# Wide products in the first half of the u stage, with the selection cut into half-microsecond steps and finished gates applied first

## The chip, the cores and the metric

The kernel runs as one program on one core of a Trainium2 chip. The metric is device time in microseconds (us) for one execution of the whole program. A core has five engines with instruction queues of their own: PE (TensorE: matrix products; its weight loads are listed as PEld), DVE (VectorE), ACT (ScalarE), POOL (GpSimd) and SP (SyncE, which issues the DMAs here). Each queue is worked off in order, and the queues wait for one another through semaphores.

## The reference, cut to what matters

Two layers run one after the other on 256 tokens of width 1024: a mixer (an SSD mixer, then a retention mixer), an expert FFN, and a gated per-layer input. The change touches the FFN alone, which is the same in both layers:

```python
def peer_ffn(h, w_q, sub_keys, u, v):
    q = (xt @ w_q).reshape(T, PEER_HEADS, 2, PEER_HALF)
    sc = jnp.einsum('thcd,hckd->thck', q, sub_keys)
    s1, i1 = lax.top_k(sc[:, :, 0], K)
    s2, i2 = lax.top_k(sc[:, :, 1], K)
    cand = (s1[..., :, None] + s2[..., None, :]).reshape(T, PEER_HEADS, K * K)
    cand_idx = (i1[..., :, None] * NK + i2[..., None, :]).reshape(T, PEER_HEADS, K * K)
    top_s, top_pos = lax.top_k(cand, K)
    idx = jnp.take_along_axis(cand_idx, top_pos, axis=-1)
    gate = jax.nn.softmax(top_s, axis=-1)
    ...
        hid = jax.nn.gelu(jnp.einsum('tkd,td->tk', u[ib], xb), approximate=False)
        return jnp.einsum('tk,tkd->td', (gb * hid).astype(xb.dtype), v[ib])
```

K is 16, NK is 128 and there are 8 heads: each token chooses 128 of 16384 experts.

## The kernel before, in words

The FFN isn't gathered. The kernel computes all 16384 products of u with every token (the u stage), multiplies them by a gate that is zero for the experts a token did not choose, and multiplies by all of v (the v stage). Float32 accuracy comes from splitting: an operand becomes a high part and a low part of a faster type, and three products are added (high x high, high x low, low x high). ACT writes the high part of a weight block (`wh`), and POOL or DVE subtracts it from the raw block to get the low part (`wl`).

`peer` holds the FFN. The **u stage** is the loop `for i in range(P)`: 128 blocks of 128 experts. A block of u comes in by four DMAs (L513), is transposed by DVE (L516, 128x1024), cast by ACT to `wh` (L521) and subtracted by POOL to `wl` (L524). PE then does 24 products of 256 columns into one PSUM tile `m`: for each of 8 chunks of the width, `wh` with `xh` (L1243) and `wh` with `xl` (L1244), then `wl` with `xh` eight times (L1247). ACT applies the Gelu in the next round (L1207) and so frees the tile; there are two `m` tiles. `get()` hands over the split block of this round and, in the same call, issues the cast and the subtraction for the next block and the load and transpose for the one after it. `wh` and `wl` have two buffers each. The transposed blocks share four raw buffers; from block 56 on (`UEND`) the DMA's target is taken from those four as well.

The first 61 blocks of a layer run beside the **selection**: DVE's top-16 search over the scores, the sums of candidates, the positions, the softmax (an Exp on ACT, L1086) and the experts' numbers. It is a list `bg` of steps with a cost in ns each; `pump(PUMP)` adds 1700 ns of credit per block and pops steps until the credit is used up. Four of the sixteen score pieces are made in rounds 0 and 1 (`score`, L1001 on PE, L1003 on ACT). When `bg` is empty, `sel_tr` turns the results over, and the second half of the u stage begins: for every four tokens `g_hot` makes one-hot tables on DVE (L1172, L1175), `g_lo` scales them on ACT (L1181), `g_mm` multiplies them on PE (L1187) into one of two `g` tiles, and `g_apply` multiplies the gates into H (L1197 on ACT, L1201 on DVE). `g_slot` moves this along by a stage per round. Where gates were there before the hidden value, `times` (L1211) multiplies them in.

The order on each engine is the order in which the Python code calls it; nothing is rearranged afterwards. So within a round before, ACT's order was: cast for the next block, then Gelu of the last block, then `g_apply`'s part, then `g_lo`.

Of the kernel before, what the change touches and what calls it, by code (L numbers as in the profile page):

```python
# [18 lines left out]
P = 128  # L19
# [5 lines left out]
GS = 4096.0  # L25
PUMP = 1700
UEND = 56
# [61 lines left out]
def trunk(ctx: ExitStack, tc: tile.TileContext, a, out, dbg=None, stop=None):  # L89
# [864 lines left out]
    def peer(l, st):  # L954
# [13 lines left out]
        tq = view(S0 + 9344, 256)  # L968
        e1 = A[:, S0 + 9856:S0 + 10368].bitcast(F16).rearrange("p (a b c) -> p a b c", a=4, b=16)
        sel = view(S0 + 10880, 4, 256)  # L970
# [34 lines left out]

        def top(src, scr, ov, oi):

            for r in range(2):
                o8 = slice(8 * r, 8 * r + 8)
                for i in range(2):  # L1010
                    dve.max(ov[i][:, o8], (src, scr)[r][i])
                for i in range(2):
                    dve.max_index(oi[i][:, o8], ov[i][:, o8], (src, scr)[r][i])
                if r == 0:
                    for i in range(2):
                        dve.match_replace(scr[i], ov[i][:, o8], src[i], NEG)

        def sel_codes(tb, c):
            u = 256 * tb + 16 * c
            top([sc[:, tb, c + i] for i in range(2)], sc2, [sv[:, tb, c + i] for i in range(2)],  # L1020
                [iu[:, u + 16 * i:u + 16 * i + 16] for i in range(2)])

        def sel_sums(tb):


            if tb == 0:
                dve.tensor_copy(io16, iota16[:, :16])
# [12 lines left out]

        def sel_cand(tb, h):
            u = 128 * tb + 16 * h
            top([cand[:, tb, h + i] for i in range(2)], cand2, [ts_[:, tb, h + i] for i in range(2)],
                [pu[:, u + 16 * i:u + 16 * i + 16] for i in range(2)])

        def sel_pos(part):

            i, j = pa[:, 0], pa[:, 1]
            if part == 0:
                dve.tensor_copy(si, iu)  # L1050
                dve.tensor_copy(B0, pu)
                dve.tensor_scalar(A2[:, 0].bitcast(U32), pu, 2, None, op0=OP.logical_shift_right)
                dve.tensor_scalar(A2[:, 1].bitcast(U32), pu, 3, None, op0=OP.logical_shift_right)
                dve.tensor_copy(pf, A2.bitcast(U32))
            if part == 1:
                dve.tensor_scalar(A2[:, 0], pf[:, 0], -6.0, 0.0, op0=OP.add, op1=OP.max)
                dve.scalar_tensor_tensor(tq, pf[:, 1], -1.0, A2[:, 0], op0=OP.add, op1=OP.max)
                dve.scalar_tensor_tensor(i, B0, -48.0, tq, op0=OP.add, op1=OP.max)
            if part == 2:
                dve.tensor_scalar(A2[:, 0], i, 8.0, 8.0, op0=OP.mult, op1=OP.add)  # L1060
                dve.tensor_scalar(A2[:, 1], i, 4.0, 24.0, op0=OP.mult, op1=OP.add)
                dve.scalar_tensor_tensor(A2[:, 0], i, 16.0, A2[:, 0], op0=OP.mult, op1=OP.min)
                dve.scalar_tensor_tensor(tq, i, 48.0, A2[:, 1], op0=OP.add, op1=OP.min)
            if part == 3:
                dve.tensor_tensor(tq, tq, A2[:, 0], op=OP.min)
                dve.tensor_sub(j, B0, tq)

        def sel_idx(tb, h, c, part):
            u = slice(128 * tb + 16 * h, 128 * tb + 16 * h + 64)
            if part == 0:  # L1070
                dve.tensor_tensor(e1, io16.unsqueeze(1).unsqueeze(1).to_broadcast([P, 4, 16, 16]),
                                  pa[:, c, u].rearrange("p (a b) -> p a b", a=4).unsqueeze(3).to_broadcast(
                                      [P, 4, 16, 16]), op=OP.is_equal)
            if part == 1:
                s4 = si.rearrange("p (t h c k) -> p t h c k", t=2, h=8, c=2)[:, tb, h:h + 4, c]
                dve.tensor_mul(e1, e1, s4.unsqueeze(2).to_broadcast([P, 4, 16, 16]))
            if part == 2:
                dve.tensor_reduce(sel[:, c, u].rearrange("p (a b) -> p a b", a=4), e1, axis=AX.X, op=OP.add)
# [42 lines left out]
        bg += [(1900, sel_pos, 0), (700, sel_gate), (1100, sel_pos, 1), (1500, sel_pos, 2), (800, sel_pos, 3)]  # L1121
        idx = [(1200, sel_idx, tb, h, c, k) for tb in range(2) for h in (0, 4) for c in range(2) for k in range(3)]
        bg += idx[:3] + [(1400, sel_sum)] + idx[3:6] + [(1000, sel_split)] + idx[6:8]
        for i in range(4):
            bg += [(600, sel_ratio, i), idx[8 + i]]
        bg += idx[12:]
        bg += [(2000, wait), (50, sel_tr, 0), (50, sel_tr, 1)]
        credit = [0.0]
# [8 lines left out]
        def q_fill(k):  # L1137
            if k < 4:
                score(k // 2, k % 2)
            if bg[0][3] < 8:  # L1140
                pump(1550)
            if k < 2:
                q_move(2 * k)
                q_move(2 * k + 1)
            if k in (4, 6):
                xh, xl = split_x(xm[:, 2 * k - 8:2 * k - 4])
                xp.extend((xh[:, i], xl[:, i]) for i in range(4))
            return 0
# [6 lines left out]
        i4 = bank[0][:, :256].bitcast(F16).rearrange("p (a b) -> p a b", b=4)  # L1155
        io16, sm = bank[0][:, 256:272], bank[0][:, 272:288]
        sv2 = bank[0][:, 384:512].rearrange("p (a b) -> p a b", a=8)
# [33 lines left out]
        def g_apply(b, ps, i):  # L1191
# [6 lines left out]
            if i:  # L1198

                for r in ((slice(0, 4), slice(4, P)) if 4 * b + 4 == T else (slice(0, i),)):  # L1200
                    dve.scalar_tensor_tensor(hv[:, r], pv[:, r], 1.0 / GS, hv[:, r], op0=OP.mult, op1=OP.mult)  # L1201
            stored[0] = 4 * b + 4

        def gelu(i, ps):
            st = stored[0]
            if st < T:
# [5 lines left out]

        def g_slot(i, times=lambda: None):

            ap, mm, lo, b = gst["ap"], gst["mm"], gst["lo"], gst["next"]
            gst.update(ap=None, mm=lo, lo=None)
# [5 lines left out]
            if ap:  # L1222
                g_apply(*ap, i)
            if lo:
                g_lo(lo[0], *lo[1])
            times()
            return ap or mm or lo

        last, since = None, 0
        for i in range(P):  # L1230
            wh, wl = get()
            if last is not None:
                g_slot(i, gelu(i - 1, last))
                if bg:
                    pump(PUMP)
                else:
                    since += 1
                    if since % 8 == 0 and T // 4 - gst["next"] > P - 1 - i:
                        g_slot(i)
# [24 lines left out]

        cur = None if open_() else wsplit(0)
        g_slot(P, gelu(P - 1, last))
        while open_():
            g_slot(P)

# [200 lines left out]
```

## Time and profile before

| what | us |
|---|---|
| runs before: median (lowest to highest of 3) | 2180.57 (2179.05 to 2184.51) |
| the profiled execution: its own time | 2179.29 |
| span of the profile | 2177.5 |
| PE busy in the span | 2124.8 |
| u stage, layer 0: first and last start of L1243 | 313.1 to 721.6 |
| v stage, layer 0: first and last start of L1281 | 723.9 to 1072.4 |

The second layer repeats the pattern from about 1371 us on. A line of the timeline gives the start, the duration, the engine, the source line, the operation, the tiles written and read, the shape and how many were merged; in brackets stands how long the engine was idle just before and what ended that. Durations contain an engine's pipeline, so the next instruction often starts before the last one ends; what an engine can do per us is read from the distance of starts.

### The profile page before, as it was taken

To read this page: it belongs to the slowest core of one execution; us is meant where nothing else is said; L and a number is where in the kernel's file an instruction comes from. 1 tells how busy PE (TensorE), PEld (TensorE's weight loads), DVE (VectorE), ACT (ScalarE), POOL (GpSimd) and SP (SyncE) were. 2 spreads that over 40 slices of the span, in tenths; PEclk is the share of its full clock that TensorE was granted. 3 is DMA by queue.
4 is the path that set the end of the run, shared out by engine and by line. 5 is a ranking of instruction groups with operands and counts; after the bars stand their busy time and mean duration, and the time that the engine had idled before them with its cause. 6 is when DMAs were issued, how large, how long until landed. Compare 5 with 4: busy or idle time off the path is not lost. (4 is left out here: it accounts for less than half of the span.)

```text
span 2177.5 us, 39792 instructions
## 1 busy us (share of the span) xinstructions
PE 2124.8 (98%) x15013; PEld 1967.9 (90%) x15013; DVE 1578.6 (72%) x2641; ACT 1207.3 (55%) x2077; POOL 833.5 (38%) x384
## 2 busy tenths in 40 slices
PE   8989999999999999999999999999999999999997
PEld 8978899999999888888898999999999998888887
DVE  7787578888999655555587366989699985555556
ACT  5654444547888544444554444445588874444445
POOL 3242258877777100000033223888777740000001
PEclk9999999999999999999999999999999999999999
DMA  5423577756555655655656456865555556655653
GB/s 185 137 78 98 166 195 194 184 135 167 155 156 154 185 194 194 194 194 193 200 176 186 130 168 184 198 184 151 157 156 156 155 169 193 194 193 194 193 190 121
DMA packets 219577, 370.27 MB, mean 170 GB/s; under 512 B 24240, under 2 KB 163192, under 8 KB 219384
## 3 DMA queue, kind: packets, MB, share of 16 engines
q1 hardware_dynamic: 219064, 367.19, 56.6%
q8 instruction: 118, 1.93, 0.4%
q14 instruction: 75, 0.61, 0.1%
q10 hardware_dynamic: 320, 0.53, 0.1%
HBM read 364.48 MB, written 1.05 MB: 168 GB/s over the span
## 5 line engine op out<-in xcount | busy, mean ns | idle before, releaser
L139 DVE TENSOR_TENSOR wl<-raw,wh 128x1024 fp32r<-128x1024 f32 x379 | 473.5, 1251 | 399.0 <-ACT wh L136 398.7
L136 ACT CAST wh<-raw 128x1024 fp32r<-128x1024 f32 x429 | 450.3, 1052 | 484.3 <-PE ps L1281 359.0
L524 POOL TENSOR_TENSOR wl<-raw,wh 128x1024 fp32r<-128x1024 f32 x256 | 618.3, 2416 | 198.6 <-ACT wh L521 191.1
L1243 PE MATMUL m<-X,wh 128*128 128x256 f32 x2048 | 513.2, 288 | 0.5 <-ACT arena L1207 0.4
L1281 PE MATMUL ps<-wh,X 128*128 128x512 f32 x2048 | 507.3, 389 | 1.9 <-ACT X L1258 1.9
L1244 PE MATMUL m<-X,wh 128*128 128x256 f32 x2048 | 502.0, 283 | 0.0
L1281 PEld LDWEIGHTS ps<-wh,X 128*128 128x128 f32 x2048 | 384.1, 188 | 82.0 <-ACT X L1258 2.3
L521 ACT CAST wh<-raw 128x1024 fp32r<-128x1024 f32 x256 | 269.1, 1051 | 263.2 <-issue 150.1
L1243 PEld LDWEIGHTS m<-X,wh 128*128 128x128 f32 x2048 | 392.2, 192 | 1.0 <-ACT arena L1207 0.9
L1244 PEld LDWEIGHTS m<-X,wh 128*128 128x128 f32 x2048 | 393.0, 192 | 0.0
L199 PE MATMUL ps<-X,wh 128*128 128x256 f32 x2368 | 331.2, 290 | 9.5 <-ACT wh L136 7.9
L341 POOL TENSOR_TENSOR arena<-arena 128x512 f32<-128x512 f32 x15 | 24.1, 1606 | 815.6 <-ACT arena L339 806.5
L199 PEld LDWEIGHTS ps<-X,wh 128*128 128x128 f32 x2368 | 303.8, 195 | 15.5 <-ACT wh L136 9.9
L1247 PE MATMUL m<-X,wl 128*128 128x256 f32 x2048 | 287.4, 283 | 0.1
L1281 PE MATMUL ps<-wl,X 128*128 128x512 f32 x1024 | 274.7, 389 | 0.0
L1247 PEld LDWEIGHTS m<-X,wl 128*128 128x128 f32 x2048 | 264.1, 192 | 0.8 <-POOL wl L524 0.7
L1281 PEld LDWEIGHTS ps<-wl,X 128*128 128x128 f32 x1024 | 192.2, 188 | 39.8
L516 DVE STREAM_TRANSPOSE raw<-raw 128x1024 f32<-128x1024 f32 x144 | 179.0, 1243 | 39.1 <-DMA raw<-in_peer_u 32.7
L139 POOL TENSOR_TENSOR wl<-raw,wh 128x1024 fp32r<-128x1024 f32 x50 | 125.2, 2510 | 182.4 <-ACT wh L136 149.9
L199 PE MATMUL ps<-X,wl 128*128 128x256 f32 x1184 | 178.9, 289 | 7.0 <-POOL wl L139 3.8
L199 PEld LDWEIGHTS ps<-X,wl 128*128 128x128 f32 x1184 | 159.6, 196 | 9.3 <-POOL wl L139 5.0
L1181 ACT ACTIVATE ol<-ol,G 128x128 f16<-128x128 f16 x512 | 162.8, 398 | 0.1
(263 smaller groups left out, 2019.3 us busy)
## 6 DMA issues: line engine op xcount, KB each, us to landing
raw<-in_peer_v SPq DMA_DIRECT2D x256, 512.0 KB, 4.3
raw<-in_peer_u SPq DMA_DIRECT2D x576, 128.0 KB, 3.0
arena<-in_peer_u SPq DMA_DIRECT2D x448, 128.0 KB, 3.3
raw<-in_ret_w_in SPq DMA_DIRECT2D x48, 512.0 KB, 4.0
raw<-in_ssd_w_in SPq DMA_DIRECT2D x41, 512.0 KB, 3.8
raw<-in_peer_w_q SPq DMA_DIRECT2D x32, 512.0 KB, 4.4
raw<-in_ssd_w_out SPq DMA_DIRECT2D x16, 512.0 KB, 3.8
raw<-in_ple_gate SPq DMA_DIRECT2D x16, 512.0 KB, 4.7
```

The lines of the kernel that those rows point to most:

```text
L136: act.copy(wh[:, :n], r[:, :n])
L139: (eng or dve).tensor_sub(wl[:, :n], r[:, :n], wh[:, :n].bitcast(F32))
L199: pe.matmul(self.t[n // 2][:, n % 2], w[:, n * P:(n + 1) * P], x, start=st, stop=sp_, skip_group_check=True)
L341: pool.tensor_add(self.sq[:, 0], self.sq[:, 0], self.sq[:, b])
L516: dve.transpose(t.rearrange("p (k b i) -> p b k i", k=8, b=4), r.rearrange("p (b k i) -> p b k i", k=8, b=4))
L521: act.copy(wh, t)
L524: pool.tensor_sub(wl, t, wh.bitcast(F32))
L1181: act.activation(hl[:, 1, j], hl[:, 0, j], AF.Copy, scale=G1[:, t:t + 1])
L1243: pe.matmul(last, wh[:, s], xh, start=k == 0, stop=False)
L1244: pe.matmul(last, wh[:, s], xl, start=False, stop=False)
L1247: pe.matmul(last, wl[:, s], xh, start=False, stop=k == KD - 1)
L1281: pe.matmul(sums[b], h[:, tb * P:(tb + 1) * P], w[:, n * 512:(n + 1) * 512], start=i == 0 and p == 0, stop=i == P - 1 and p == 2)
```

## The change

In the first half of the u stage (`wide`, while `bg` holds steps) the 16 products of `wh` become 8 of 512 columns, against `xh` and `xl` side by side; the eight of `wl` stay. The two halves of the PSUM tile must then be added: ACT copies the right half to H (L1249 of the changed file), DVE adds the left half (L1250), and the Gelu runs one round later on H in place (L1252). These three, and in the second half the Gelu and `g_apply` and `times` (`g_done`), now stand ahead of `get()`. The selection's steps are cut into pieces, `PUMP` goes from 1700 to 1180, and the experts' numbers come from 32 fused operations and 12 sums of 512 elements in the place of 24 operations on 1024. `warm` loads the Exp table ahead of the Exp.

```diff
-PUMP = 1700
+PUMP = 1180
...
-        def sel_idx(tb, h, c, part):
-            u = slice(128 * tb + 16 * h, 128 * tb + 16 * h + 64)
-            if part == 0:
-                dve.tensor_tensor(e1, io16.unsqueeze(1).unsqueeze(1).to_broadcast([P, 4, 16, 16]),
...
+        def sel_idx(c, r0):
+
+
+            v = pa[:, c].rearrange("p (h k) -> p h k", k=16)
+            for r in (r0, r0 + 1):
+                k = slice(r if c else r // 8 * 8, 16)
+                n = 16 - k.start
+                s1 = si.rearrange("p (h c k) -> p h c k", c=2, k=16)[:, :, c, r:r + 1]
+                dve.scalar_tensor_tensor(e1[:, r, :, k], v[:, :, k], float(r), s1.to_broadcast([P, 16, n]),
+                                         op0=OP.is_equal, op1=OP.mult)
+
+        def sel_add(c, i, h):
+
+            h = slice(h, h + (8, 4)[i])
+            dve.tensor_reduce(sel[:, c].rearrange("p (h k) -> p h k", k=16)[:, h, 8 * i:8 * i + 8],
+                              e1[:, :8 * i + 8, h, 8 * i:8 * i + 8].rearrange("p r h k -> p h k r"), axis=AX.X, op=OP.add)
...
+            act.activation(warm, ident[:, :1], AF.Exp)
...
-        bg = [(3100, sel_codes, tb, c0 + c) for c0 in (0, 8) for tb in range(2) for c in range(0, 8, 2)]
+        bg = [(n, sel_codes, tb, c0 + c, i) for c0 in (0, 8) for tb in range(2) for c in range(0, 8, 2)
+              for i, n in enumerate((400, 520, 520, 400, 520))]
         for tb in range(2):
-            bg += [(1800, sel_sums, tb)]
-            bg += [(2500, sel_cand, tb, h) for h in range(0, 8, 2)]
...
+            bg += [(1300, sel_sums, tb)]
+            bg += [(n, sel_cand, tb, h, i) for h in range(0, 8, 2) for i, n in enumerate((270, 330, 330, 270, 330))]
...
-        last, since = None, 0
+        last, since, wide, late = None, 0, False, None
         for i in range(P):
+            if wide:
+                act.copy(H[:, i - 1], last[:, T:])
+                dve.tensor_add(H[:, i - 1], last[:, :T], H[:, i - 1])
+            if late is not None:
+                act.activation(H[:, late], H[:, late], AF.Gelu)
+            late = i - 1 if wide else None
+            if last is not None:
+                times = gelu(i - 1, last) if not wide else lambda: None
+                g_done(i)
+                times()
             wh, wl = get()
             if last is not None:
-                g_slot(i, gelu(i - 1, last))
+                g_slot()
                 if bg:
                     pump(PUMP)
...
-            last = mis.tile([P, 512], F32, name="m")[:, :T]
-            for k, (xh, xl) in enumerate(xp):
+            last = mis.tile([P, 512], F32, name="m")
+
+            wide = bool(bg)
+            for k, (xh, xl, xx) in enumerate(xp):
                 s = slice(k * P, (k + 1) * P)
-                pe.matmul(last, wh[:, s], xh, start=k == 0, stop=False)
-                pe.matmul(last, wh[:, s], xl, start=False, stop=False)
-            for k, (xh, xl) in enumerate(xp):
+                if wide:
+                    pe.matmul(last, wh[:, s], xx, start=k == 0, stop=k == KD - 1, skip_group_check=True)
+                else:
+                    pe.matmul(last[:, :T], wh[:, s], xh, start=k == 0, stop=False)
+                    pe.matmul(last[:, :T], wh[:, s], xl, start=False, stop=False)
+            for k, (xh, xl, xx) in enumerate(xp):
                 s = slice(k * P, (k + 1) * P)
-                pe.matmul(last, wl[:, s], xh, start=False, stop=k == KD - 1)
+                pe.matmul(last[:, :T], wl[:, s], xh, start=False, stop=k == KD - 1, skip_group_check=wide)
```

How it moves the instructions is seen at three places. First, ACT at the Exp of the selection in layer 0. Before:

```order
L521 CAST wh<-raw 128x1024
L1207 ACTIVATE arena<-m 128x256
L1086 ACT_TABLE_LOAD
L1086 ACTIVATE arena<-arena 128x256
L521 CAST wh<-raw 128x1024
L1207 ACT_TABLE_LOAD
L1207 ACTIVATE arena<-m 128x256
L521 CAST wh<-raw 128x1024
```

And now, at the same place (L1249 is the copy of the right half, L1252 the late Gelu):

```order
L521 CAST wh<-raw 128x1024
L1091 ACT_TABLE_LOAD
L1091 ACTIVATE warm<-ident 128x1
L1094 ACTIVATE arena<-arena 128x256
L1249 COPY arena<-m 128x256
L1252 ACT_TABLE_LOAD
L1252 ACTIVATE arena<-arena 128x256
L521 CAST wh<-raw 128x1024
L1249 COPY arena<-m 128x256
L1252 ACTIVATE arena<-arena 128x256
L521 CAST wh<-raw 128x1024
```

The cast stood between Exp and the Gelu's table load; now the copy, the table load and the Gelu stand ahead of it, as in every round the copy and the Gelu do.

Second, ACT at the first rounds of the u stage as it now is:

```order
L521 CAST wh<-raw 128x1024
L1003 COPY arena<-g 128x512 x2
L1249 COPY arena<-m 128x256
L1252 ACT_TABLE_LOAD
L1252 ACTIVATE arena<-arena 128x256
L521 CAST wh<-raw 128x1024
L1249 COPY arena<-m 128x256
```

Here too the load of the Gelu's table, which stood behind a cast, is ahead of one.

Third, DVE in the second half. Before, a round was transpose, one-hot tables, then the gates:

```order
L516 STREAM_TRANSPOSE raw<-raw 128x4x8x32
L1172 TENSOR_TENSOR oh<-ps,G_98 128x1024
L1175 TENSOR_TENSOR ol<-oh,ps 128x512
L1201 SCALAR_TENSOR_TENSOR arena<-g,arena 128x83x4
L1211 TENSOR_TENSOR arena<-arena,m 128x72
```

The instructions are the same now, but a round begins with the gates:

```order
L1215 SCALAR_TENSOR_TENSOR arena<-g,arena 128x83x4
L1225 TENSOR_TENSOR arena<-arena,m 128x72
L516 STREAM_TRANSPOSE raw<-raw 128x4x8x32
L1186 TENSOR_TENSOR oh<-ps,G_98 128x1024
L1189 TENSOR_TENSOR ol<-oh,ps 128x512
```

On PE nothing changes place: both programs turn the selection over (`sel_tr`) after 61 blocks of a layer, and both multiply the first gates ahead of block 64.

## Rows read from the trace of the kernel before

**Rows 1.** The page, part 1: busy us, share of the span, instructions.

```profile
PE 2124.8 (98%) x15013; PEld 1967.9 (90%) x15013; DVE 1578.6 (72%) x2641; ACT 1207.3 (55%) x2077; POOL 833.5 (38%) x384
```

**Rows 2.** Windows, layer 0's first half: us; PE, PEld, DVE, ACT, POOL busy; clock; DMA.

```profile
313.10:487.80 174.70, 174.70 (x1460) 174.70 (x1459) 152.42 (x458) 84.84 (x125) 142.83 (x60) 1.00 0.66 171
```

**Rows 3.** Timeline of PE: narrow products, first half of the u stage.

```profile
480.01 1.12 PE L1247 MATMUL m<-X,wl 128*128 128x256 f32 x8
...
488.65 1.12 PE L1247 MATMUL m<-X,wl 128*128 128x256 f32 x8
```

**Rows 4.** Timeline of PE: the v stage's last twelve products of 512 columns.

```profile
1069.95 0.62 PE L1281 MATMUL ps<-wh,X 128*128 128x512 f32 x2
...
1072.67 0.64 PE L1319 MATMUL g<-X,wh 128*128 128x256 f32 x4
```

**Rows 5.** Waits, 485 to 540 us, and 1545 to 1600 alike: total, times, longest.

```profile
PE g L1187 <- DVE arena L1201: 1.6, 1, 1.6
```

**Rows 6.** Timeline, first half: ACT's cast, then POOL's subtraction.

```profile
370.81 1.05 ACT L521 CAST wh<-raw 128x1024 fp32r<-128x1024 f32 x1 [1.55 <-issue]
...
371.94 2.41 POOL L524 TENSOR_TENSOR wl<-raw,wh 128x1024 fp32r<-128x1024 f32 x1 [0.47 <-ACT wh L521]
```

**Rows 7.** Timeline at the u stage's end: ACT waits for PE.

```profile
721.80 1.12 PE L1247 MATMUL m<-X,wl 128*128 128x256 f32 x8
722.96 0.17 ACT L1207 ACTIVATE arena<-m 128x4 f32<-128x4 f32 x1 [2.72 <-PE m L1247]
```

**Rows 8.** Timeline: PE's weight load waits for POOL.

```profile
489.90 2.39 POOL L524 TENSOR_TENSOR wl<-raw,wh 128x1024 fp32r<-128x1024 f32 x1 [1.92 <-ACT wh L521]
...
492.35 1.02 PEld L1247 LDWEIGHTS m<-X,wl 128*128 128x128 f32 x8 [0.22 <-POOL wl L524]
```

**Rows 9.** Timeline of ACT: two reads of PSUM, one behind the other.

```profile
508.25 0.37 ACT L1207 ACTIVATE arena<-m 128x256 f32<-128x256 f32 x1
508.52 0.37 ACT L1197 ACTIVATE arena<-g 128x252 f32<-128x252 f32 x1
```

**Rows 10.** Timeline of ACT at the selection's Exp.

```profile
425.30 0.42 ACT L1086 ACTIVATE arena<-arena 128x256 f32<-128x256 f32 x1
425.62 1.03 ACT L521 CAST wh<-raw 128x1024 fp32r<-128x1024 f32 x1
426.67 1.28 ACT L1207 ACT_TABLE_LOAD   x1
427.96 0.38 ACT L1207 ACTIVATE arena<-m 128x256 f32<-128x256 f32 x1
```

**Rows 11.** Timeline, round 2: last score copy; low products of block 2.

```profile
322.77 0.59 ACT L1003 COPY arena<-g 128x512 f32<-128x512 f32 x1 [0.31 <-PE g L1001]
...
324.49 1.12 PE L1247 MATMUL m<-X,wl 128*128 128x256 f32 x8
```

**Rows 12.** Timeline of DVE: sums, transpose, a candidates' step (378.93 to 380.67).

```profile
376.32 0.29 DVE L1029 COPY ps<-arena 128x128 f32<-128x128 f32 x1
...
377.77 1.23 DVE L516 STREAM_TRANSPOSE raw<-arena 128x1024 f32<-128x1024 f32 x1
378.93 0.31 DVE L1011 MAX8 arena<-arena 128x8 f32<-128x64 f32 x2
...
380.67 1.23 DVE L516 STREAM_TRANSPOSE raw<-arena 128x1024 f32<-128x1024 f32 x1
```

**Rows 13.** Timeline of DVE: 256 columns out of PSUM, then a transpose.

```profile
434.80 0.43 DVE L1093 TENSOR_TENSOR ps<-arena,ps 128x256 f32<-128x256 f32 x1
435.14 1.24 DVE L516 STREAM_TRANSPOSE raw<-arena 128x1024 f32<-128x1024 f32 x1
```

**Rows 14.** Lines of DVE, 300 to 510 us: one of the three selections' operations.

```profile
L1078 DVE TENSOR_REDUCE arena<-arena 128x64 f32<-128x1024 f16 x8 | 9.5, 1191 | 0.0
```

**Rows 15.** Timeline of DVE past block 56: transposes that wait for their DMA.

```profile
487.45 1.25 DVE L516 STREAM_TRANSPOSE raw<-raw 128x1024 f32<-128x1024 f32 x1 [0.72 <-DMA raw<-in_peer_u]
...
493.31 1.25 DVE L516 STREAM_TRANSPOSE raw<-raw 128x1024 f32<-128x1024 f32 x1 [0.59 <-DMA raw<-in_peer_u]
```

More of the change, by code (lines that the diff above doesn't have):

```diff
@@ L1003, in score, with top, sel_codes @@
             act.copy(sc[:, tb, 4 * c4:4 * c4 + 4], ps.rearrange("p (a b) -> p a b", a=4))
[L1006 to L1010, printed above, removed]
+        def top(src, scr, ov, oi, part):
+            r = part // 3
+            o8 = slice(8 * r, 8 * r + 8)
+            for i in range(2):
+                if part % 3 == 0:
                     dve.max(ov[i][:, o8], (src, scr)[r][i])
-                for i in range(2):
+                elif part % 3 == 1:
                     dve.max_index(oi[i][:, o8], ov[i][:, o8], (src, scr)[r][i])
[L1014 to L1018, printed above, removed]
+                else:
+                    dve.match_replace(scr[i], ov[i][:, o8], src[i], NEG)
+        def sel_codes(tb, c, part):
             u = 256 * tb + 16 * c
             top([sc[:, tb, c + i] for i in range(2)], sc2, [sv[:, tb, c + i] for i in range(2)],
-                [iu[:, u + 16 * i:u + 16 * i + 16] for i in range(2)])
+                [iu[:, u + 16 * i:u + 16 * i + 16] for i in range(2)], part)
         def sel_sums(tb):
-            if tb == 0:
-                dve.tensor_copy(io16, iota16[:, :16])
             v = sv[:, tb].rearrange("p (h c) k -> p h c k", c=2)
@@ L1039, in sel_sums, with sel_cand @@
                         dve.tensor_add(dst[:, :, i * nj:(i + 1) * nj], v1[:, :, i:i + 1].to_broadcast([P, 8, nj]), v2)
-        def sel_cand(tb, h):
+        def sel_cand(tb, h, part):
             u = 128 * tb + 16 * h
             top([cand[:, tb, h + i] for i in range(2)], cand2, [ts_[:, tb, h + i] for i in range(2)],
-                [pu[:, u + 16 * i:u + 16 * i + 16] for i in range(2)])
+                [pu[:, u + 16 * i:u + 16 * i + 16] for i in range(2)], part)
         def sel_pos(part):
@@ L1051, in sel_pos @@
                 dve.tensor_copy(B0, pu)
+            if part == 4:
                 dve.tensor_scalar(A2[:, 0].bitcast(U32), pu, 2, None, op0=OP.logical_shift_right)
@@ L1061, in sel_pos @@
                 dve.tensor_scalar(A2[:, 1], i, 4.0, 24.0, op0=OP.mult, op1=OP.add)
+            if part == 5:
                 dve.scalar_tensor_tensor(A2[:, 0], i, 16.0, A2[:, 0], op0=OP.mult, op1=OP.min)
@@ L1066, in sel_pos @@
                 dve.tensor_sub(j, B0, tq)
-        def sel_idx(tb, h, c, part):
-            u = slice(128 * tb + 16 * h, 128 * tb + 16 * h + 64)
-            if part == 0:
-                dve.tensor_tensor(e1, io16.unsqueeze(1).unsqueeze(1).to_broadcast([P, 4, 16, 16]),
[L1072 to L1078, printed above, removed]
+        def sel_idx(c, r0):
[10 more added lines that the diff above has]
+                              e1[:, :8 * i + 8, h, 8 * i:8 * i + 8].rearrange("p r h k -> p h k r"), axis=AX.X, op=OP.add)
+        warm = small.tile([P, 1], F32, name="warm", bufs=1)
         def sel_gate():
@@ L1115, in wait @@
             pass
[L1117 removed]
+        bg = [(n, sel_codes, tb, c0 + c, i) for c0 in (0, 8) for tb in range(2) for c in range(0, 8, 2)
+              for i, n in enumerate((400, 520, 520, 400, 520))]
         for tb in range(2):
[L1119 to L1123 removed]
+            bg += [(1300, sel_sums, tb)]
+            bg += [(n, sel_cand, tb, h, i) for h in range(0, 8, 2) for i, n in enumerate((270, 330, 330, 270, 330))]
+        bg += [(900, sel_pos, 0), (600, sel_gate), (1100, sel_pos, 4), (1200, sel_pos, 1), (850, sel_pos, 2),
+               (850, sel_pos, 5), (800, sel_pos, 3)]
+        idx = [[], []]
+        for c, cost in ((0, (660,) * 4 + (400,) * 4), (1, (660, 620, 560, 480, 420, 350, 290, 220))):
+            idx[c] += [(n, sel_idx, c, 2 * i) for i, n in enumerate(cost)]
+            idx[c] += [(650, sel_add, c, 0, h) for h in (0, 8)] + [(650, sel_add, c, 1, h) for h in range(0, 16, 4)]
+        bg += idx[0][:4] + [(1200, sel_sum)] + idx[0][4:8] + [(1100, sel_split)] + idx[0][8:]
         for i in range(4):
[L1125 to L1127 removed]
+            bg += [(750, sel_ratio, i)] + idx[1][2 * i:2 * i + 2]
+        bg += idx[1][8:]
+        bg += [(1300, wait), (50, sel_tr, 0), (50, sel_tr, 1)]
         credit = [0.0]
@@ L1145, in q_fill @@
             if k in (4, 6):
+                both = X[:, xn[0] % 3]
                 xh, xl = split_x(xm[:, 2 * k - 8:2 * k - 4])
-                xp.extend((xh[:, i], xl[:, i]) for i in range(4))
+                xp.extend((xh[:, i], xl[:, i], both[:, :, i]) for i in range(4))
             return 0
@@ L1155, in peer @@
         i4 = bank[0][:, :256].bitcast(F16).rearrange("p (a b) -> p a b", b=4)
-        io16, sm = bank[0][:, 256:272], bank[0][:, 272:288]
+        sm = bank[0][:, 272:288]
         sv2 = bank[0][:, 384:512].rearrange("p (a b) -> p a b", a=8)
@@ L1198, in g_apply @@
             if i:
-                for r in ((slice(0, 4), slice(4, P)) if 4 * b + 4 == T else (slice(0, i),)):
+                for r in ((slice(0, 4), slice(4, i)) if 4 * b + 4 == T else (slice(0, i),)):
                     dve.scalar_tensor_tensor(hv[:, r], pv[:, r], 1.0 / GS, hv[:, r], op0=OP.mult, op1=OP.mult)
@@ L1211, in gelu, with g_done, g_slot @@
             return lambda: dve.tensor_mul(H[:, i, :st], H[:, i, :st], ps[:, :st])
-        def g_slot(i, times=lambda: None):
-            ap, mm, lo, b = gst["ap"], gst["mm"], gst["lo"], gst["next"]
-            gst.update(ap=None, mm=lo, lo=None)
+        def g_done(i):
+            ap = gst["ap"]
+            gst["ap"] = None
+            if ap:
+                g_apply(*ap, i)
+        def g_slot():
+            mm, lo, b = gst["mm"], gst["lo"], gst["next"]
+            gst.update(mm=lo, lo=None)
             if mm:
@@ L1265, in peer @@
         cur = None if open_() else wsplit(0)
-        g_slot(P, gelu(P - 1, last))
+        times = gelu(P - 1, last)
+        g_done(P)
+        times()
+        g_slot()
         while open_():
-            g_slot(P)
+            g_done(P)
+            g_slot()
         sums = [acc.tile([P, 512], F32, name="ps") for _ in range(4)]
```

14 lines of the change are left out of this document (6 added, 8 removed).

## The prediction

> **What bounds the kernel now.** I read the page's shares first, then the windows of the u stage, the timelines of PE, ACT and DVE in it, and the waits at its seams. The page says that PE is busy 98% of the span [rows 1], and in layer 0's first half of the u stage PE has no gap at all while DVE is busy 152.4 of 174.7 us [rows 2]. So a saving on PE counts in full here, as long as no other engine becomes the later one. What PE needs is read from starts: the low products of blocks three apart start 8.64 us apart, 2.880 per block of 24, 0.120 each [rows 3]. The v stage's last twelve products of 512 columns take 2.72 us, 0.2267 each, three in a row into one PSUM bank [rows 4]. The granted clock is 1.00, the level of 2.4 GHz [rows 2].
>
> **What the change takes away.** A pair of narrow products at 2 x 0.120 becomes one wide one at 0.2267: 0.0133 us less. Both programs have 61 such blocks per layer, 8 pairs in each, 976 pairs in all: 13.0 us. A wide block then takes 8 x 0.2267 + 8 x 0.120 = 1.814 + 0.960 = 2.774 us.
>
> The row says 0.0133 per pair. The Trainium skill ("TensorE: Matmul & The Clock Gate", section "Back-to-back issue gap") gives an isolated gap of 262 cycles for 256 columns and 518 for 512, so that widening would save 6 cycles per pair, an estimated 2.4 us in all in the place of 13.0, and the whole sum would come out about 3 us slower. No row here has a narrow product at its 109 ns: the trace differs from the page, and the measured 0.120 decides.
>
> At the seam to the second half PE waits 1.6 us once for `g_apply` (L1201), which must free a `g` tile [rows 5], and the second layer's waits have the same line. DVE reaches it behind a transpose of 1.25 us [rows 12] and two one-hot operations. With the gates first in DVE's round it is sooner by all three, so both waits go: 3.3 us by the unrounded 1.64. For the rest of the second half I cost the new order at nothing: DVE and ACT do the same instructions in the same round, and PE needs what now comes later, the tables and `g_lo`'s results, only at the head of the next block. Were that cover too short, each of 64 rounds per layer would pay. Sum of the gains: 16.3.
>
> **What it adds to ACT's turn.** This is the part to watch. Before, ACT cast block i+1 as soon as PE had left the `wh` buffer. Now the cast stands behind the copy of block i-1, which waits for that block's end, and a Gelu. I count from S, PE's first product of block i. ACT follows PE's end at S + 0.20 (last low product starts at 722.64, the next would at 722.76, ACT at 722.96) [rows 7]. A 256-column read of PSUM holds ACT for 0.27 before the next starts [rows 9], one of SBUF for 0.32 [rows 10]. The cast takes 1.05, POOL starts 0.08 after its end and takes 2.41 [rows 6]. PE's weight load follows POOL's end by 0.06 [rows 8], the product by another 0.11. Sum: S + 4.50. PE wants these low products at the end of the next block's wide part, S + 2.774 + 1.814 = S + 4.59. So the new turn fits, with 0.09 us to spare, where the old cast had not waited for a block's end at all. I cost it at nothing in an ordinary round.
>
> It doesn't fit where ACT loads a table. A load takes 1.28 [rows 10]. Before, both loads at the Exp were hidden, since the cast stood between them and had slack. Now:
> - *First Gelu of a layer.* The last score copy starts 0.20 into block 2 (PE's 16 `wh` products before 324.49 began at 322.57) and holds ACT for 0.49 [rows 11]. Copy of block 1 to its end 0.38, load 1.28, Gelu 0.32, cast 1.05, POOL 2.41 and the small steps between end at S + 6.42 against S + 4.59: PE waits 1.83, twice 3.7.
> - *The Exp.* From S: copy, Gelu and cast end at 1.84, load, `warm` and Exp at about 3.6, the next copy ends at 3.98, the Gelu's load at 5.28, its Gelu hands over at 5.62, cast 6.67, POOL 9.16, product 9.33. PE wants it at 2 x 2.774 + 1.814 = 7.36: a wait of 1.97, twice 3.9. Each product waits once; afterwards the turn is in step again.
>
> **What it adds to DVE.** From the 152.4 busy us of the half [rows 2] go 22 operations on 1024 elements at 1.19 [rows 14] (the three kinds are alike): 26. To it come 61 additions out of PSUM at 0.34 [rows 13], 21; the sums of 512 elements, 12 at half of 1.19, 7; the 32 fused operations, 16 to 256 elements, about 8 by the same 0.34 for 256; and some 2.5 that the q stage now leaves over. Together 165 of 61 x 2.774 = 169. Known from both sides: a sum of 512 strided elements can't be dearer than the 1.19 of 1024; at that bound it adds 7 us per layer and DVE would be late for some rounds. I take the half, since the count of elements is halved. A round of DVE can be late by about 1.3 us before the cast must wait: copy's end 0.65, addition 0.34, transpose 1.25 make S + 2.24, and the next round's cast wants it at 2.774 + 0.79. Most rounds hold 1.2 to 1.45 us of steps. One is worse: a candidates' piece and `sel_sums` (1.45, [rows 12]) fall together, about 2.5 after three rounds that were already late by 0.35; I put 0.25 per layer, 0.5 in all.
>
> **What it adds at block 56.** From here the DMA's target shares the raw buffers, and transposes two blocks apart start 5.86 us apart, the DMA being what they wait for [rows 15]. Two blocks were 5.76 and are now 5.55. Over eight blocks that lacks 1.2 us, of which the slack eats most: 0.4 per layer, 0.8.
>
> **Sum.** Gains 16.3; losses 3.7 + 3.9 + 0.5 + 0.8 = 8.9; net 7.4 us less. The profiled execution took 2179.3, which gives 2171.9. The runs shown have a median 1.3 above it, so I predict a median of **2173.2**, 0.34% less. About 0.3%, 6.5 us, is what a measurement of this kernel can tell from no change; the forecast is just past it.
>
> **Rivals.**
> - *The two table waits are smaller or covered*, as both were before. For it: ACT is busy only 85 of 175 us [rows 2]. Against it: the order puts both ahead of a cast with 0.09 of slack. The time: 2173.2 - 7.6 = 2165.6. Chance 0.14.
> - *ACT's turn sets the period (the slower side).* Place: every wide block. The turn and the 0.96 of low products that it ends in make 5.46 us per two blocks against PE's 5.55. The gain is used up when the turn is 0.2 longer. If copy and Gelu cost their whole 0.38 and 0.42, and ACT follows PE at 0.24, it is 5.71, 2.86 per block: 122 x 0.08 = 10 us, time 2183; with another 0.2 for a Gelu that finds its addition late, 2.96 per block and 2195. Against it: rows 9 and 10 show the overlap. Chance 0.22, about half of it within 0.3%.
> - *DVE becomes the bound*, if sums and fused operations cost the upper bounds: 8 us more, 2181. Chance 0.08.
> - *Widening saves nothing*, a wide product taking the 0.240 of two narrow ones, if it is more than its columns that narrow ones wait for. Then only the seam is gained, 2180.6 - 3.3 + 8.9 - about 1 for the longer block's slack = 2185. Rows 3 and 4 speak against it. Chance 0.04. (The Trainium skill's isolated gap, above, would end near here too.)
>
> **How the numbers follow.** The forecast has 0.52, with a range of its own of 2167 to 2178 (each wait uncertain by half a microsecond, twice, and the turn's spare 0.09 as likely 0.05 short, which costs 3). Of it 0.32 lies under 2174.0. Faster by over 0.3%: 0.32 + 0.14 = 0.46. Slower by over 0.3%: half of ACT's turn and a little of DVE's, 0.13. Within: 0.41. The range 2164 to 2184 reaches over the first rival and the lower half of ACT's.
>
> **What would show it.** Right: in the first half, low products of neighbouring blocks start 2.77 us apart; PE waits about 1.8 us for `wl` in the third or fourth block and about 2.0 just past the Exp; the wait for `g_apply` is gone. Wrong: a spacing of 2.8 or more with POOL back to back and PE waiting for `wl` in every block (the turn); PE waiting for a cast that waits for a transpose while DVE never idles (DVE); wide products 0.24 apart; or no wait of PE at the table loads.

## The result and the profile after

Six runs of the changed kernel have a median of **2191.73 us** (2188.42 to 2196.24), six of the kernel before beside them 2179.95 (2178.57 to 2184.51). The ratio is 1.0053 (95% interval 1.0040 to 1.0066): slower by half a per cent, where 2173.2 had been forecast. The profiled execution took 2188.42 with a span of 2186.6.

The page's first part, in the columns of [rows 1]:

```profile
PE 2116.8 (97%) x14037; PEld 1913.7 (88%) x14037; DVE 1614.2 (74%) x2801; ACT 1246.7 (57%) x2201; POOL 833.6 (38%) x384
```

PE does 976 instructions fewer and is busy 8.0 us less, yet the span is 9.1 longer: what was saved came back as idle time, and more. Where, the starts tell: the u stage runs from its first `wh` product to the first product of the v stage. Before (products of one line: count, duration, first and last start):

```profile
L1243 PE MATMUL m<-X,wh x1024: 278/283/387, 313.2 to 721.6; 128*128 128x256 f32 x171
...
L1281 PE MATMUL ps<-wh,X x814: 389/389/497, 723.9 to 999.9; 128*128 128x512 f32 x163
```

And after:

```profile
L1274 PE MATMUL m<-X,wh x488: 387/393/504, 309.2 to 496.2; 128*128 128x512 f32 x163
...
L1318 PE MATMUL ps<-wh,X x805: 389/389/499, 726.9 to 999.9; 128*128 128x512 f32 x161
```

That is 410.7 us before and 417.7 after, 7.0 more; the second layer's stage went from 411.4 to 417.5, 6.1 more. (The 4 us by which this profile's u stage begins sooner are mostly there at 104 us already, in stages that the change doesn't touch.) The waits of PE in layer 0's u stage:

```profile
PE m L1274 <- DVE arena L1250: 8.9, 7, 2.6
PE m L1274 <- ACT wh L521: 1.7, 2, 0.9
PE ps L1318 <- ACT X L1291: 1.0, 1, 1.0
PE m L1280 <- POOL wl L524: 0.7, 2, 0.4
```

Four things are to be seen. `g_apply` is no longer among them: the seam's wait of [rows 5] is gone. The waits for a cast and for `wl` are the two table loads. The one line that nobody had forecast at this size is L1250, the addition that empties a wide block's PSUM tile, with 8.9 us. And it lies in one stretch only, as the windows show (columns of [rows 2]):

```profile
309.20:494.60 185.40, 174.10 (x994) 151.16 (x993) 175.43 (x541) 104.97 (x186) 143.38 (x61) 1.00 0.60 163
320.00:420.00 100.00, 98.83 (x565) 86.47 (x564) 96.06 (x399) 59.04 (x108) 84.61 (x36) 1.00 0.68 182
420.00:495.00 75.00, 64.87 (x362) 55.21 (x361) 71.81 (x118) 40.67 (x71) 53.56 (x23) 1.00 0.50 141
```

Up to 420 us PE loses 1.2 of 100 us, then 10 of 75 (1.3 of them at the Exp's table load). The timeline of PE and DVE where it begins, with the fused operations of `sel_idx` (L1076):

```profile
439.23 2.00 PE L1274 MATMUL m<-X,wh 128*128 128x512 f32 x8
439.84 4.55 DVE L1076 SCALAR_TENSOR_TENSOR arena<-arena,ps 128x256 f16<-128x256 f32 x4
...
444.03 0.60 DVE L1250 TENSOR_TENSOR arena<-m,arena 128x256 f32<-128x256 f32 x1
...
444.78 2.08 PE L1274 MATMUL m<-X,wh 128*128 128x512 f32 x8 [2.60 <-DVE arena L1250]
```

Four fused operations of 256 elements hold DVE from 439.84 to 444.03, 1.05 us each, about 4 ns an element. The addition stands behind them, and PE behind the addition. There are seven waits of this kind in layer 0 and six in layer 1. Added up from the starts of the blocks, which should be 2.79 apart, they put 10.7 and 10.8 us on the two layers; this is more than the idle time, because an idle stretch is counted only from the modelled end of the product before it. The delay is local: DVE still idles 10 of the 185.4 us, but from 439.84 to 445.69, where its next fused operation starts, four fused operations, one addition and one transpose take 5.85 us of a period of 2.79.

The lines of DVE, 300 to 520 us, name the group and its price:

```profile
L1250 DVE TENSOR_TENSOR arena<-m,arena 128x256 f32<-128x256 f32 x61 | 26.8, 440 | 8.3 <-ACT arena L1249 8.1
...
L1076 DVE SCALAR_TENSOR_TENSOR arena<-arena,ps 128x256 f16<-128x256 f32 (+15 forms) x32 | 24.3, 1014 | 0.0
L1082 DVE TENSOR_REDUCE arena<-arena 128x32 f32<-128x512 f16 (+1 forms) x12 | 7.4, 663 | 0.0
```

The sums of 512 elements (L1082) cost 7.4 where 7 had been put down, the 32 fused operations 24.3 where "about 8" had.

### The profile page after: what moved, and what is told of

It is laid out like the page before. It is cut to its first block, busy times and chain, and to the rows that moved or that the text cites. A ratio compares the mean times of both kernels' runs of the same rounds, so it can differ in the third digit from the quotient of the medians.

```text
span 2186.6 us, 37854 instructions
## 1 busy us (share of the span) xinstructions
PE 2116.8 (97%) x14037; PEld 1913.7 (88%) x14037; DVE 1614.2 (74%) x2801; ACT 1246.7 (57%) x2201; POOL 833.6 (38%) x384
## 3 DMA queue, kind: packets, MB, share of 16 engines
HBM read 364.48 MB, written 1.05 MB: 167 GB/s over the span
## 5 line engine op out<-in xcount | busy, mean ns | idle before, releaser
L1280 PEld LDWEIGHTS m<-X,wl 128*128 128x128 f32 x2048 | 270.4, 191 | 13.8 <-POOL wl L524 5.1
L1276 PE MATMUL m<-X,wh 128*128 128x256 f32 x1072 | 273.0, 293 | 0.0
L1274 PE MATMUL m<-X,wh 128*128 128x512 f32 x976 | 247.6, 396 | 19.9 <-DVE arena L1250 16.0
L1277 PE MATMUL m<-X,wh 128*128 128x256 f32 x1072 | 262.2, 282 | 0.0
L1274 PEld LDWEIGHTS m<-X,wh 128*128 128x128 f32 x976 | 176.2, 190 | 54.9 <-issue 11.6
L1277 PEld LDWEIGHTS m<-X,wh 128*128 128x128 f32 x1072 | 205.0, 191 | 0.0
L1276 PEld LDWEIGHTS m<-X,wh 128*128 128x128 f32 x1072 | 204.5, 191 | 0.3
```

Source lines behind the costliest of these rows:

```text
L1274: pe.matmul(last, wh[:, s], xx, start=k == 0, stop=k == KD - 1, skip_group_check=True)
L1276: pe.matmul(last[:, :T], wh[:, s], xh, start=k == 0, stop=False)
L1277: pe.matmul(last[:, :T], wh[:, s], xl, start=False, stop=False)
L1280: pe.matmul(last[:, :T], wl[:, s], xh, start=False, stop=k == KD - 1, skip_group_check=wide)
```

## The experiments

The open question was why 256 elements take 1.05 us there and 0.34 in [rows 13]. Three differences offered themselves: the layout of the table that they fill (`e1`: for one position its 2-byte results lie 32 bytes apart), the operation, and its broadcast operand `si` in PSUM. Beside that, the table loads, the widening and the short steps were each to be measured alone. All medians stand against the kernel before that ran with them: 2178.08 beside experiments 1, 2, 4 and 6, 2179.67 beside 5, 7, 8 and 9, 2179.27 beside 3 and 10. The changed kernel ran only beside the 2179.95 above.

**1. Results side by side.**

```
-        e1 = A[:, S0:S0 + 2048].bitcast(F16).rearrange("p (h k r) -> p r h k", h=16, k=16)
+        e1 = A[:, S0:S0 + 2048].bitcast(F16).rearrange("p (r h k) -> p r h k", h=16, k=16)
```

> The changed kernel with one word of layout: the table that the 32 fused operations of a layer fill is stored position by position, so that a fused operation writes its 2-byte results side by side and the sums read them with a step. In the changed kernel's trace those operations stand 1.05 us apart for 256 elements, about 4 ns an element, and the additions of the wide blocks, queued behind them, hold TensorE back by 10.7 us per layer. Theory A (2-byte results written 32 bytes apart are what costs): 256 elements fall to 0.35 to 0.6 us, TensorE's waits for the addition go, and the time is 2191.7 - 2 x 10.7 = 2170 (2168 to 2174). Theory B (the operation itself is slow, whatever the layout): still 1.05 us and 2190 to 2193. Theory C (its broadcast operand in PSUM is what costs): the same as B. If reading with a step costs in the sums instead, they grow from 0.66 us towards 2 us and the time lies between, about 2180.

Measured: 2176.83, ratio 0.9994 (0.9985 to 1.0004). Lines of DVE, same stretch:

```profile
L1082 DVE TENSOR_REDUCE arena<-arena 128x32 f32<-128x512 f16 (+1 forms) x12 | 12.3, 1069 | 0.0
L1076 DVE SCALAR_TENSOR_TENSOR arena<-arena,ps 128x256 f16<-128x256 f32 (+15 forms) x32 | 8.1, 308 | 0.0
```

And four operations of 256 elements on the timeline, with the addition behind them:

```profile
446.58 1.38 DVE L1076 SCALAR_TENSOR_TENSOR arena<-arena,ps 128x256 f16<-128x256 f32 x4
447.88 0.42 DVE L1250 TENSOR_TENSOR arena<-m,arena 128x256 f32<-128x256 f32 x1
```

They are 0.33 us apart (1.30 for four) instead of 1.05. The same operation with the same operands takes 8.1 us a layer, the prediction's "about 8", once its results lie side by side. So the layout costs, not the operation (theory B) nor the operand in PSUM (C). The sums, which now read with a step of 512 bytes, grew from 0.66 to 1.07 us each and hold some of the gain back: the blocks' starts slip by 3.5 us per layer instead of 10.7 (1.4 and 1.9 of it are there in experiment 2 too, from another cause), and the time lies between the two that were expected.

**2. The same order in four bytes.**

```
-        e1 = A[:, S0:S0 + 2048].bitcast(F16).rearrange("p (h k r) -> p r h k", h=16, k=16)
+        e1 = view(S0, 4096).rearrange("p (h k r) -> p r h k", h=16, k=16)
```

> The changed kernel with the same table, in the same order, kept in four bytes instead of two: results of a fused operation now lie 64 bytes apart and each is a whole word. Theory A1 (writing half a word at a time is what costs): the fused operations fall to 0.35 to 0.6 us for 256 elements and the time to about 2170. Theory A2 (the step between results is what costs, of any width): still about 1.05 us and 2190 or more. Theories B and C (the operation, or its operand in PSUM): also 1.05 us and about 2191.

Measured: 2172.66, ratio 0.9978 (0.9968 to 0.9988).

```profile
L1076 DVE SCALAR_TENSOR_TENSOR arena<-arena,ps 128x256 f32<-128x256 f32 (+15 forms) x32 | 10.8, 443 | 0.0
L1082 DVE TENSOR_REDUCE arena<-arena 128x32 f32<-128x512 f32 (+1 forms) x12 | 7.4, 658 | 0.0
```

```profile
441.23 1.98 DVE L1076 SCALAR_TENSOR_TENSOR arena<-arena,ps 128x256 f32<-128x256 f32 x4
443.03 0.43 DVE L1250 TENSOR_TENSOR arena<-m,arena 128x256 f32<-128x256 f32 x1
```

Twice the bytes, twice the step, and less than half the time: operations of 256 elements stand 0.45 us apart (1.80 for four; the 0.49 of later expectations counts the last one's tail). A2 (a step of any width) is out as the main cost. What the step adds to whole words is not measured by itself: between this 0.45 and the 0.33 of experiment 1 both width and step differ. What is left of the slip, 1.4 and 1.9 us, has another cause, seen in this run's timeline of DVE and PE:

```profile
476.23 1.25 DVE L516 STREAM_TRANSPOSE raw<-raw 128x1024 f32<-128x1024 f32 x1 [2.23 <-DMA raw<-in_peer_u]
...
478.85 0.42 DVE L1250 TENSOR_TENSOR arena<-m,arena 128x256 f32<-128x256 f32 x1
...
479.41 2.06 PE L1274 MATMUL m<-X,wh 128*128 128x512 f32 x8 [1.01 <-DVE arena L1250]
```

Past block 56 a transpose waits for its DMA, and the addition stands behind the transpose.

**3. Two bytes, each in a word of its own.** Between 2 and the changed kernel two things differ, width and step. Here only the width does:

```
-        e1 = A[:, S0:S0 + 2048].bitcast(F16).rearrange("p (h k r) -> p r h k", h=16, k=16)
+        e1 = A[:, S0:S0 + 4096].bitcast(F16).rearrange(
+            "p (h k r w) -> p r h k w", h=16, k=16, w=2)[:, :, :, :, 0]
```

> The changed kernel with the table of the fused operations still in two bytes and in the same order, but each result in a four-byte place of its own, so that results lie 64 bytes apart as they do in the four-byte table. Between the two-byte table (32 bytes apart, 1.05 us for 256 elements) and the four-byte one (64 bytes apart, 0.49 us) two things differ, the width of a result and the step. Theory (the width: a result of half a word, standing alone, is what costs): still about 1.05 us, TensorE's waits for the addition as before, 2189 to 2194. Rival (the step: results 32 bytes apart meet each other, 64 bytes apart they do not): about 0.5 us and 2171 to 2175.

Measured: 2191.78, ratio 1.0054 (1.0034 to 1.0074).

```profile
L1076 DVE SCALAR_TENSOR_TENSOR arena<-arena,ps 128x256 f16<-128x256 f32 (+15 forms) x32 | 25.2, 1049 | 0.0
```

At the step of experiment 2 the 2-byte results are as slow as in the changed kernel, and so is the kernel. It is the width of a result that stands alone.

**4. The codes in SBUF.**

```
-        si = bank[1]
+        si = view(S0 + 9856, 512)
```

> The changed kernel with the codes that the fused operations multiply by kept in SBUF instead of a PSUM bank. Theory C (the broadcast operand in PSUM is what costs): 256 elements fall from 1.05 us to 0.35 to 0.6 and the time to about 2170. Theories A and B (the layout of the results, or the operation itself): still 1.05 us apart and 2190 to 2193.

Measured: 2225.51, ratio 1.0217 (1.0202 to 1.0233): no theory had a time over 2193. The timeline of POOL and DVE:

```profile
438.52 2.41 POOL L524 TENSOR_TENSOR wl<-raw,wh 128x1024 fp32r<-128x1024 f32 x1 [0.36 <-ACT wh L521]
439.12 5.78 DVE L1076 SCALAR_TENSOR_TENSOR arena<-arena 128x256 f16<-128x256 f32 x2
441.32 2.50 POOL L524 TENSOR_TENSOR wl<-raw,wh 128x1024 fp32r<-128x1024 f32 x1 [0.38 <-ACT wh L521]
...
453.79 2.42 DVE L1076 SCALAR_TENSOR_TENSOR arena<-arena 128x256 f16<-128x256 f32 x2
```

Two operations take 5.78 us while POOL splits weights. From 453.79 on, with POOL idle at first, two are through in 2.02 (the next starts at 455.81), close to the 1.05 each of the changed kernel. So the operand in PSUM costs nothing (theory C falls again); in SBUF it brings in POOL.

**5. The same with the table in four bytes**, to part POOL's share from the slow writes.

> The changed kernel with the table in four bytes and the codes in SBUF instead of PSUM. With the codes in SBUF and the table in two bytes two operations took 5.78 us where GpSimd was splitting weights beside them, and 2.02 us where it was not, and the kernel took 2225. Theory (a fused operation with both inputs in SBUF stands still while GpSimd works): here too pairs that fall beside GpSimd's 2.4 us operations are held, TensorE waits for additions from 440 us on, and the time is 2180 to 2205, well over the 2172.7 of the four-byte table with the codes in PSUM. Rival (the 2225 came of the slow writes alone, which got worse): 2171 to 2175.

Measured: 2205.52, ratio 1.0114 (1.0098 to 1.0130), at the upper end of what the theory allowed. Two operations beside POOL, and two alone:

```profile
438.17 2.40 POOL L524 TENSOR_TENSOR wl<-raw,wh 128x1024 fp32r<-128x1024 f32 x1 [0.38 <-ACT wh L521]
438.75 2.74 DVE L1076 SCALAR_TENSOR_TENSOR arena<-arena 128x256 f32<-128x256 f32 x2
...
448.89 1.03 DVE L1076 SCALAR_TENSOR_TENSOR arena<-arena 128x256 f32<-128x256 f32 x2
450.17 2.39 POOL L524 TENSOR_TENSOR wl<-raw,wh 128x1024 fp32r<-128x1024 f32 x1 [3.50 <-ACT wh L521]
```

2.74 against 1.03, with the table fast: an operation with both inputs in SBUF stands still until POOL's ends at 440.57; the pair ends 0.92 later, about its time alone. The two costs are independent: the codes in SBUF add some 33 us over the slow table and over the fast one (2225.5 against 2191.7, 2205.5 against 2172.7, medians of different batches). The Trainium skill ("SBUF — State Buffer", section "SBUF: two separate sides") says this: a VectorE operation with two SBUF inputs and a GpSimd operation that reads SBUF need the same pair of ports, and whichever starts second is blocked for the whole of the other. The rows agree.

**6. The finished Gelu behind the cast.** The changed kernel with its slow table, and in `peer`'s loop:

```
-            if late is not None:
-                act.activation(H[:, late], H[:, late], AF.Gelu)
-            late = i - 1 if wide else None
             if last is not None:
...
             wh, wl = get()
+            if late is not None:
+                act.activation(H[:, late], H[:, late], AF.Gelu)
+            late = i - 1 if wide else None
```

> The changed kernel with ScalarE's finished Gelu of a block placed behind the cast of the next weights instead of ahead of it, so that the two table loads of a layer (the first Gelu, and the return to Gelu after the Exp) no longer stand between an eviction and the cast that TensorE waits for. In the changed kernel's trace the starts of the blocks slip by 1.82 us at the first Gelu and 1.78 us at the Exp. My theory (these waits are the loads, and nothing else is late there): both go, 3.6 us per layer and 7.2 in all, 2184.5 (2183 to 2187). Rival (VectorE, which lags later, gives the time back: a TensorE that is earlier only waits longer for the additions): the wait at the Exp comes back in the waits from 444 us on, 2186 to 2189. Rival (the order on ScalarE does not matter, the cast waits for something else): 2191 to 2193.

Measured: 2184.94, ratio 1.0036 (1.0022 to 1.0050): 6.9 us over the kernel before beside it, where the changed kernel was 11.8 over its own. PE's waits, 305 to 500 us:

```profile
PE m L1274 <- DVE arena L1250: 7.4, 6, 2.5
PE ps L199 <- POOL wl L139: 0.7, 1, 0.7
```

The waits for the cast and for `wl` are gone, the waits for additions stay. The slips at the two table loads fell from 1.82 and 1.78 us to 0.22 and 0.24. The two first halves together are 5.8 us shorter by the starts of their blocks, not 7.2: the slips behind the additions grew by 0.1 and 0.4, so the loads are the main cause of these waits, and the first rival takes back a little.

**7. Both repairs together**, experiments 2 and 6.

> The table of the fused operations in four bytes and the finished Gelu behind the cast, both together. The two costs lie at different blocks (320 to 326 us and 423 to 431 us for the Gelu, from 439 us on for the fused operations), so they should add: 2172.7 of the four-byte table alone less 2 x 3.0 (the two slips of 1.82 and 1.78 us became 0.22 and 0.24 behind the cast, and the blocks after it gave a little back) = 2166.5 (2164.5 to 2168.5). Rival: what is won at the Gelu is lost again to the transfer that comes late near 475 us, which a TensorE that is 3 us earlier meets sooner: 2169 to 2172.

Measured: **2165.69**, ratio **0.9931** (0.9915 to 0.9946). The stretch of layer 0 that was the changed kernel's first half (here block 61 already starts at 487.6), and PE's waits from 305 to 740 us:

```profile
309.20:495.00 185.80, 185.19 (x1097) 163.31 (x1096) 172.38 (x552) 111.43 (x201) 154.61 (x64) 1.00 0.67 175
```

```profile
PE ps L1318 <- ACT X L1291: 1.0, 1, 1.0
PE ps L199 <- POOL wl L139: 0.7, 1, 0.7
PE m L1274 <- DVE arena L1250: 0.6, 1, 0.6
```

PE is busy 185.2 of 185.8 us, with DVE at 172.4 beside it. The two costs add as expected, and this version is faster than both kernels.

**8. Widening undone in it.**

```
-            wide = bool(bg)
+            wide = False
```

> The same with the 61 wide blocks of a layer written as narrow products again (256 columns for the high and 256 for the low part), without the copy and the addition that the wide form needs; the order of finished gates and the short selection steps stay. The price of widening by itself: a wide block's start follows the one before by 2.794 us, a narrow block's by 24 x 0.120 = 2.880, so 61 x 0.086 = 5.2 us per layer and 10.5 in all are given up: 2166.5 + 10.5 = 2177 (2175 to 2179), which is the kernel before less its two seam waits of 1.64 us. Rival (widening saves nothing): 2166 to 2168. Rival (the additions and copies of wide blocks cost TensorE more than the products save): below 2166.

Measured: 2176.25, ratio 0.9984 (0.9973 to 0.9994). Widening is worth 10.6 us here; 61 blocks a layer at 0.086 make 10.5.

**9. Widening undone in the changed kernel**, slow table and all (the same line).

> The changed kernel with narrow products in the selection's blocks and nothing else altered: the fused operations stay at their slow 1.05 us for 256 elements, but no block waits for an addition any more, since ScalarE evicts it alone. Theory (the slow operations reach TensorE only because the additions stand behind them on VectorE's queue): TensorE's waits of 10.7 us per layer go, and the time is that of the narrow kernel with the fast table, about 2177 (2175 to 2180). Rival (VectorE is also late with the transposes of the next weights, so the lag reaches TensorE by that way): TensorE waits for casts from 440 us on and the time is 2182 or more.

Measured: 2176.58, ratio 0.9982 (0.9972 to 0.9993). Its fused operations are as slow as ever (1394 ns on average for 256 elements, 1383 in the changed kernel), and PE's waits in the same stretch as in 6 are these:

```profile
PE m L1280 <- POOL wl L524: 0.9, 3, 0.3
PE ps L199 <- POOL wl L139: 0.7, 1, 0.7
PE m L1276 <- ACT wh L521: 0.3, 1, 0.3
```

One of the short waits is at the Exp's table load (437.4 us), 0.7 us belong to the stage before, and the other three are past 490 us, where transposes also wait for their DMA. Narrow blocks also take the 61 additions off DVE, about 21 us a layer, so DVE has less to do here in all. But at the slow operations it falls behind here too: two neighbouring transposes start 5.6 us apart (440.54 and 446.15), while the casts stay 2.88 apart (441.80, 444.68, 447.56). Up to block 56 a late transpose is taken in, and the slow operations reach PE by the additions alone.

The time is 3.1 us under the kernel before. This is not a price of the new order of gates: in the profiled executions the two u stages together are as long as before (821.8 against 822.0 us). The order itself shows in the starts: from block 61 (counted from 0, the first behind the selection) to the v stage each layer takes 1.6 us less, 3.2 in all where the two seam waits had been put at 3.3. The first halves lose most of it again, 0.9 us a layer at the Exp's table load.

**10. Short steps undone** in the version of 7.

```
+        bg = [(2360, whole(sel_codes), tb, c0 + c) for c0 in (0, 8) for tb in range(2) for c in range(0, 8, 2)]
...
+            bg += [(1530, whole(sel_cand), tb, h) for h in range(0, 8, 2)]
```

(`whole` calls the five parts one after the other.)

> The four-byte table and the Gelu behind the cast, with the 24 selection steps of a layer's codes and candidates in one piece again (2.4 and 1.5 us, as in the kernel before) instead of five steps of 0.3 to 0.5 us each; all else alike. Theory (from the trace of the kernel with short steps: an addition ends 1.6 us before TensorE needs its tile, a transpose some 1.1 us before its cast would start later): two blocks hold 2 x 1.16 of transposes, 2 x 0.34 of additions and one step of 2.36, 5.36 of 5.59 us; the addition behind a whole step is then about 1.06 us late, inside the 1.6, and TensorE waits little: 2166 to 2170. Rival (short steps are what keeps the additions in time): each of the 16 long steps of a layer puts 0.5 us or more on TensorE, 2180 or more.

Measured: 2165.18, ratio 0.9933 (0.9916 to 0.9950), the same as with short steps. PE's waits for additions are 0.7 and 1.3 us in the two layers against 0.6 and 0.9. A long step makes an addition late, and the block after it catches up: one starts at 336.06 us, 1.4 behind its copy, and ends at 336.46, PE needs its tile at 337.23, and the next (337.83) follows its copy by 0.4. In this kernel the short steps of codes and candidates carry nothing.

## Why the prediction was wrong

**What held.** The seam: both waits are gone, and from block 61 to the v stage the changed kernel takes 1.2 and 1.9 us less than before, 3.0 of the 3.3. ACT's turn in an ordinary round: no wait of PE for a cast or for `wl` outside the table loads, so the likeliest rival, ACT's turn as the period with 2183 to 2195, was not the mechanism; that the time fell into its range is chance. The table loads: 1.82 and 1.78 us in layer 0 against 1.83 and 1.97, and both go when the load stands behind the cast (PE stood first at `wh`, 0.8 and 0.9, and only then at `wl`, which alone had been named). Additions (0.34 apart) and sums (7.4 against 7): as put down.

**What was a little off.** A wide block follows the one before by 2.794 us instead of 2.774. Low products start 2.79 to 2.80 apart, in the timeline of PE of the changed kernel:

```profile
405.76 1.12 PE L1280 MATMUL m<-X,wl 128*128 128x256 f32 x8
406.71 2.00 PE L1274 MATMUL m<-X,wh 128*128 128x512 f32 x8
408.56 1.11 PE L1280 MATMUL m<-X,wl 128*128 128x256 f32 x8
```

Eight wide products take 1.85 us, 0.231 each, where [rows 4] had 0.2267: 61 x 0.086 = 5.2 us saved per layer, not 6.5. The 0.25 for `sel_sums` did not show. The 0.4 per layer at block 56 was hidden behind the larger wait. When that was gone (experiment 2) the blocks there lost 1.4 and 1.9, and since the kernel before itself loses 0.6 and 1.0 in the same blocks, the term was 0.8 and 0.9.

**The step that failed** is in the part on DVE: "the 32 fused operations, 16 to 256 elements, about 8 by the same 0.34 for 256". They cost 24.3. The 0.34 was read from an operation that writes whole words side by side, and was carried over to one that writes half words apart; the new layout of `e1`, a line of the change, was left without a price. The text had an upper bound for the sums but none for these.

The 16 us too few are not simply added to a full engine, for DVE idled 10 us in the same half. They fall together. The kernel's own step list has the same wrong price, 660 ns for two operations of 256 elements that take 2.1 us, so `pump` set four of them, 4.2 us, between two additions. The path was wrong too: the prediction let a late DVE reach PE through the transpose and the cast, with about 1.3 us to spare, where it came through the addition that empties the PSUM tile. So the mechanism was that of the third rival, "DVE becomes the bound", in a stretch of blocks and not over the whole half. It had been given a chance of 0.08 and 2181, because 7 of its 8 us were the sums', and the sums cost what had been put down.

**The sum again, with measured terms**, per layer: products -5.2, seam -1.6, table loads +3.6, additions held up +10.7 and +10.8. The last hold what the kernel before itself loses in the blocks past 56, -0.6 and -1.0. Together that is +6.9 and +6.6, where the stages show +7.0 and +6.1; half a microsecond of the second layer stays open.

## What to carry to other kernels

Before an operation is priced by another of the same size, compare how both lay out their results: width and step count, not elements alone. Where a store is changed so that a later reduction reads in order, price both ends (here 8.1 + 12.3, 24.3 + 7.4 or 10.8 + 7.4 us a layer, by layout). When an engine is forecast to have 4 us of slack in 169, every term on it needs its own upper bound. And a sum over a whole stretch does not show where the work falls: an engine that idles 10 of 185 us can still hold up another, if four slow operations stand in front of the one that is waited for.

## What the runs showed of the hardware

- In the fused operations of VectorE, 2-byte results that stand alone cost about 4.1 ns each, 32 or 64 bytes apart alike (32 operations: 24.3 and 25.2 us); side by side 1.3 (0.33 us for 256); 4-byte results 64 bytes apart 1.8 (0.45).
- A sum over 512 elements takes 0.66 us when it reads 2-byte values in order, 2-byte values 4 bytes apart, or 4-byte values in order; 1.07 when it reads 2-byte values 512 bytes apart.
- An operation on VectorE with both inputs in SBUF stands still while GpSimd splits weights from SBUF (2.74 against 1.03 us for two); with one of them in PSUM four took 1.80 us beside GpSimd (experiment 2, 441.23 us), the 0.45 each that two with both in SBUF take alone.
